# PEER stage: a comparison row in PSUM, 42 instead of 28 expert products made ahead, a quarter of the gated one-hots in VectorE alone

## The chip, the cores and the metric

The kernel runs on one core of a Trainium2 chip. The metric is the device time of one execution in microseconds (us), the median of three runs. TensorE multiplies matrices (PE in the rows, PEld for its weight loads), VectorE is DVE, ScalarE is ACT, GpSimd is POOL, and SyncE (SP) issues most of the DMAs. SBUF is the working memory of the engines, PSUM the memory that TensorE writes to, in eight banks.

## The reference, cut to what matters

The program is a transformer of several blocks over 512 tokens with 1024 features. Only its last layer, `peer_ffn`, is touched by the change:

```
q  = n @ w_q                      # 8 heads, 2 halves of 128
s  = q . sub_keys                 # 128 keys per head and half
s1, i1 = top_k(s[:, :, 0], 16);  s2, i2 = top_k(s[:, :, 1], 16)
cand   = s1 + s2 (16 x 16);      top_s, pos = top_k(cand, 16)
idx    = i1[...] * 128 + i2[...]  # one of 16384 experts
gate   = softmax(top_s)
act    = gelu(expert_u[idx] . n)
out    = sum over 8 heads x 16 experts of gate * act * expert_v[idx]
```

So each token takes 128 of 16384 experts, and the sum of their value rows is weighted with gate times activation.

## The kernel before, in words

The 512 tokens are handled in two ways. For the first 384 (`TD`, three blocks of 128, `ND` = 3) the layer is computed densely: all 16384 experts are gone through in 128 tiles of 128 (`NE`). For the last 128 tokens the rows of the chosen experts are fetched one by one with indirect DMAs. Everything is in float32. A matmul of float32 operands is made of three passes over a high and a low half (`acc3`, L154 to L160), so each weight tile is split on arrival (`wload`, L143, with `split`, L139): ScalarE copies the high half (L140), VectorE or GpSimd subtracts it for the low half (L141).

The layer has three stages.

- *Routing* (`route`, L1448 to L1532). For each head and half, TensorE makes the query (24 matmuls of 512 columns) and the scores, VectorE picks the best 16 (`top16`, L1397), combines the candidates (`second`, L1449) and recovers the chosen index: it compares positions with a row of numbers `iof` (L1474), GpSimd multiplies by the candidate index (L1476), VectorE sums (L1487).
- *Gates* (`gates`, L1537 to L1568). A matrix of gates, expert by token, is built for the 384 tokens. For each token two one-hot rows of 128 are made on VectorE by comparing the row `iof` with a token's index (L1548), in groups of four tokens, 96 groups in all; one of them is multiplied by the gate, on GpSimd in three groups of four (L1550) and on ScalarE in the fourth (L1553); TensorE multiplies the two (L1555) into PSUM tile `g`, ScalarE copies it out (L1559), and twelve DMAs on SP's queue store the gates to DRAM as `Gd` (L1563).
- *Gather* (`gather`, L1570 to L1698). For each expert tile i, `v_tile` (L1635) multiplies the expert product `hb` by the gates (L1649), splits the result, and TensorE accumulates it with the value weights into six PSUM banks (`v_block`, 18 matmuls of 512 columns, `acc`). Every fourth tile the next block of gates is loaded into the only buffer `g` (L1641). Row fetches for the last 128 tokens run beside it: an indirect DMA (L1612), a dot product (L1618) and a weighted addition (L1624) on VectorE. How many fetches go with a step follows from `done` (L1671): a step that has an expert product counts twice.

An *expert product* is `h_tile` (L1427): 24 matmuls of 384 columns on PSUM tiles `o` and `t` in turn, then a gelu on ScalarE (L1439). Products for i below `NA` = 10 stay in `early`, up to `NH` = 22 in twelve `hb` buffers; the next `NX` = 6 go through two buffers `away` to DRAM (L1441) and are loaded back in the gather stage (`h_back`, L1443). These 28 are made ahead: `NR` = 14 in the routing stage, one for each of the first 14 half heads, after the half head's scores, and 14 in the gates stage, one or two after every 32 tokens. The other 100 are made in the gather stage, each three steps (`LAG`) ahead of its v tile. Weights of products made ahead are split by GpSimd, the others by VectorE.

Each engine works through its own queue in order. The order on each queue is fixed when the program is built, and it is not quite that of the source: matmuls of an expert product stand between those of other tiles, and some products of the gates loop already lie in the routing stage. Weights are loaded through four buffers (`wr`) and split into four (`ws`), so a load can run up to four tiles ahead.

PSUM use: two banks for `o` and `t` throughout, four more in routing, four in the gates, six in the gather stage.

Of the kernel before, what the change touches and what calls it, by code (L numbers as in the profile page):

```python
# [56 lines left out]
class Net:  # L57
# [1348 lines left out]

    def peer(self, st):
        nc, V, S, G, T, I = self.nc, self.V, self.S, self.G, self.T, self.I
        ND, NE, NA, NH, NX, NR, NS = 3, 128, 10, 22, 6, 14, 4
        TD = ND * 128  # L1410
        u, rest, ws = self.start(st)
        pp = self.ctx.enter_context(self.tc.tile_pool(name="peer", bufs=1))
# [30 lines left out]
        def h_back(i):  # L1443

            hbs[i] = dn.tile([128, TD], F32, name="hb", bufs=NH - NA)
            nc.sync.dma_start(hbs[i], hs[i - NH])

        with self.phase("route") as rp, self.banks(mm=2, s=2):  # L1448
            def second(h, v16, i16):  # L1449

                if16 = rp.tile([128, 4, 2, 16], F32, name="if16", bufs=2)
                V.tensor_copy(if16, i16)
                V.tensor_scalar(if16[:, :, 0], if16[:, :, 0], 128.0, None, OP.mult)
                cs = rp.tile([128, 4, NCAND], F32, name="cs", bufs=2)
                ci = rp.tile([128, 4, NCAND], F32, name="ci", bufs=2)
                off = 0
                for i0, ni, nj in CAND:
                    n = ni * nj
                    for dst, src, e in ((cs, v16, V), (ci, if16, G)):
                        o = dst[:, :, off:off + n].rearrange("p h (a b) -> p h a b", b=nj)  # L1460
                        a_ = src[:, :, 0, i0:i0 + ni, None].to_broadcast([128, 4, ni, nj])
                        b_ = src[:, :, 1, None, 0:nj].to_broadcast([128, 4, ni, nj])
                        e.tensor_tensor(o, a_, b_, OP.add)
                    off += n
                tsc = rp.tile([128, 4, 16], F32, name="tsc", bufs=2)
                tpi = rp.tile([128, 4, 16], U32, name="tpi", bufs=2)
                for tb in range(4):
                    self.top16(tsc[:, tb], tpi[:, tb], cs[:, tb], NCAND)
                tpf = rp.tile([128, 4, 16], F32, name="tpf", bufs=2)
                V.tensor_copy(tpf, tpi)  # L1470
                eqs = []
                for tb in range(4):
                    eq = rp.tile([128, 16, NCAND], F32, name="eq", bufs=4)
                    V.tensor_tensor(eq, tpf[:, tb, :, None].to_broadcast([128, 16, NCAND]),  # L1474
                                    iof[:, None, 0:NCAND].to_broadcast([128, 16, NCAND]), OP.is_equal)
                    G.tensor_tensor(eq, eq, ci[:, tb:tb + 1].to_broadcast([128, 16, NCAND]), OP.mult)  # L1476
                    eqs.append(eq)
                g = gate[:, :, h]
                V.tensor_tensor(g, tsc, tsc[:, :, 0:1].to_broadcast([128, 4, 16]), OP.subtract)
                S.activation(g, g, AF.Exp)  # L1480
                gs = self.sm.tile([128, 4], F32, name="gs")
                V.tensor_reduce(gs, g, AX.X, OP.add)
                V.reciprocal(gs, gs)
                V.tensor_tensor(g, g, gs[:, :, None].to_broadcast([128, 4, 16]), OP.mult)
                yield
                for tb, eq in enumerate(eqs):
                    V.tensor_reduce(idf[:, tb, h], eq, AX.X, OP.add)  # L1487
                    yield

            late = []  # L1490
            Ps = [self.pt("mm"), self.pt("s")[:, 0:TD], self.pt("mm"), self.pt("s")[:, 0:TD]]
            first = self.gemm_first(ws, u, rest, (T_, TD, T_, TD), Ps)
            for h in range(8):
                v16 = rp.tile([128, 4, 2, 16], F32, name="v16", bufs=2)
                i16 = rp.tile([128, 4, 2, 16], U32, name="i16", bufs=2)
                for p in range(2):
                    j = 2 * h + p
                    key = rp.tile([128, 128], F32, name="key", bufs=2)
                    nc.sync.dma_start(key, I["keysT"][:, j * 128:(j + 1) * 128])
                    P = first.pop(0) if first else self.gemm_a([(I["peer_w_q"][j], 8)], u, G)  # L1500
                    hP = first.pop(0) if first else None
                    q = self.tmp.tile([128, T_], F32, name="qT", tag="sw", bufs=2)
                    S.activation(q, P, AF.Copy)
                    P = self.pt("s", (128, 4, 128))
                    for tb in range(4):
                        T.matmul(P[:, tb], q[:, tb * 128:(tb + 1) * 128], key, start=tb == 0, stop=tb == 3,
                                 skip_group_check=True)
                    sc = rp.tile([128, 4, 128], F32, name="sc", bufs=3)
                    S.activation(sc, P, AF.Copy)
                    for tb in range(4):  # L1510
                        self.top16(v16[:, tb, p], i16[:, tb, p], sc[:, tb], 128)
                    if p == 0 and late:
                        self.weave(late.pop())
                    if j < NR:
                        h_tile(j, hP)
                late.append(second(h, v16, i16))
                next(late[0])
            ei = rp.tile([128, 2, ND, NE], I32, name="ei", bufs=1)
            ef = rp.tile([128, 2, ND, NE], F32, name="ef", bufs=1)
            for tb in range(4):  # L1520
                next(late[0])
                e = ei[:, 0, tb] if tb < ND else idx
                V.tensor_copy(e, idf[:, tb].rearrange("p b c -> p (b c)"))
                if tb == ND:
                    break
                V.tensor_scalar(ei[:, 1, tb], e, 127, None, OP.bitwise_and)
                V.tensor_scalar(e, e, 7, None, OP.logical_shift_right)
                V.tensor_copy(ef[:, :, tb], ei[:, :, tb])
                P = self.pt("s", (128, 3, 128))
                for j in range(3):  # L1530
                    T.transpose(P[:, j], ef[:, j, tb] if j < 2 else gate[:, tb].rearrange("p a b -> p (a b)"), self.idf)
                S.activation(eT[:, :, tb * 128:tb * 128 + 128], P, AF.Copy)  # L1532
# [4 lines left out]
        with self.phase("gates") as rp, self.banks(g=4):  # L1537
            nh = NR
            for t0 in range(0, TD, 32):
                for t1 in range(0, 32, 8):  # L1540
                    P = self.bank[0].tile([128, 8, 128], F32, name="g", tag="g", bufs=2)
                    for k in range(0, 8, 4):
                        t = t0 + t1 + k
                        o = [self.tmp.tile([128, 4, 128], F32, name="o0", tag="tmp"),
                             rp.tile([128, 4, 128], F32, name="o1", bufs=4)]
                        col = lambda x: x[:, t:t + 4, None].to_broadcast([128, 4, 128])
                        for i in (1, 0):
                            V.tensor_tensor(o[i], iof[:, None].to_broadcast([128, 4, 128]), col(eT[:, i]), OP.is_equal)  # L1548
                        if t // 4 % NS:
                            G.tensor_tensor(o[1], o[1], col(gT), OP.mult)  # L1550
                        else:
                            for x in range(4):
                                S.activation(o[1][:, x], o[1][:, x], AF.Copy, scale=gT[:, t + x:t + x + 1])  # L1553
                        for x in range(4):
                            T.matmul(P[:, k + x], o[1][:, x], o[0][:, x], start=True, stop=True)  # L1555
                    if t1 == 0:
                        st = [rp.tile([128, 64, 32], F32, name="gst", bufs=3) for i in range(2)]
                    for i in range(2):
                        S.activation(st[i][:, :, t1:t1 + 8].rearrange("p a t -> p t a"),  # L1559
                                     P[:, :, i * 64:i * 64 + 64], AF.Copy)  # L1560
                S.activation(g_now[:, t0 // 32], st[0][:, 0:4], AF.Copy)
                for i in range(2):
                    nc.sync.dma_start(Gd[t0 // 32, i * 16:i * 16 + 16].rearrange("a b t -> b a t"),  # L1563
                                      st[i].rearrange("p (a x) t -> p a (x t)", x=4))
                n1 = NR + (NH + NX - NR) * (t0 // 32 + 1) // (TD // 32)
                for i in range(nh, n1):
                    h_tile(i)
                nh = n1  # L1568

        with self.phase("gather") as gp, self.banks(acc=6):  # L1570

            def nrm(*todo):
# [332 lines left out]
```

## Time and profile before

| | |
|---|---|
| median of three runs | 4230.45 us (4223.23 to 4231.51) |
| the profiled execution | 4224.36 us, span of its instructions 4222.5 us |
| routing, from 2832 to 3058 us | 226 us |
| gates, from 3058 to 3250 us | 192 us |
| gather, from 3250 to 4195 us, and the end to 4222.5 us | 945 and 27.5 us |

The profile is of one execution. "Busy" counts the time in which an engine runs an instruction; a wait inside an instruction counts as busy, and a matmul's recorded duration is longer than its distance from the next, since matmuls overlap. "Idle before" is the time an engine stood still before an instruction, put down to whatever ended last. [...] The boundaries of the stages above are read from the order of the instructions.

### The profile page before, as it was taken

The numbers are of one execution on the slowest core, as the hardware profiler recorded it, in microseconds if no ns is written. First come the engines' busy times: TensorE is split into PE (matmuls) and PEld (weight loads), VectorE is DVE, ScalarE is ACT, GpSimd is POOL, SyncE is SP. The second block draws the span as 40 slices with busy tenths as digits, with TensorE's granted clock in tenths as the row PEclk, the third lists the DMA queues.
The fourth block names the chain that finished last, engine by engine and source line by source line (L and its number), as shares of the span: only waits on it lengthen the run. The fifth ranks groups of instructions, "written<-read, shape, count | busy, mean of one in ns | idle before, by whom it ended". The sixth has DMA issues, their size and how long they took to land.

```text
span 4222.5 us, 54408 instructions
## 1 busy us (share of the span) xinstructions
PE 4015.4 (95%) x20388; PEld 3411.3 (81%) x20388; DVE 2822.3 (67%) x5043; ACT 1675.7 (40%) x3108; POOL 768.6 (18%) x573
## 2 busy tenths in 40 slices
PE   7999999999999999999999999798778999999999
PEld 5888789998888888885568889587667799999998
DVE  7556655666654575557664337969998777777777
ACT  3224443444322332245553224443366433433333
POOL 2001211110000100013010004337764011111111
PEclk9999999999999999999999999899999999999999
DMA  6654222322454446540023324032256788888886
GB/s 239 191 185 138 86 75 75 90 78 67 136 186 155 129 136 189 185 129 28 1 70 128 102 86 138 29 108 85 74 146 197 252 313 304 296 306 297 308 298 228
DMA packets 267896, 661.18 MB, mean 157 GB/s; under 512 B 24048, under 2 KB 126960, under 8 KB 250864
## 3 DMA queue, kind: packets, MB, share of 16 engines
q1 hardware_dynamic: 249200, 523.48, 38.5%
q0 software_dynamic: 18432, 134.23, 8.7%
q8 instruction: 160, 2.62, 0.3%
q14 instruction: 104, 0.85, 0.1%
HBM read 624.86 MB, written 32.77 MB: 156 GB/s over the span
## 4 chain that ended last, share of the span: by engine, by line
PE 75%; DVE 16%; issue 5%; DMA 2%; ACT 1%; POOL 1%; SPq 0%; DVEq 0%; ACTq 0%; POOLq 0%
PE mm L156 15%; PE mm L160 14%; PE mm L159 14%; PE acc L160 4%; PE acc L159 4%; PE acc L156 4%; DVE o L1548 3%; PE o L1104 2%; DVE cv L1242 2%; PE t L160 2%; PE t L156 2%; PE t L159 2%; PE o L160 2%; PE o L156 2%; PE o L159 2%
## 5 line engine op out<-in xcount | busy, mean ns | idle before, releaser
L141 DVE TENSOR_TENSOR wspl<-wraw,wspl 128x1024 fp32r<-128x1024 f32 (+3 forms) x695 | 787.1, 1135 | 707.1 <-ACT wspl L140 702.6
L140 ACT ACTIVATE wspl<-wraw 128x1024 fp32r<-128x1024 f32 (+3 forms) x757 | 746.4, 987 | 1156.7 <-PE mm L160 523.0
L156 PE MATMUL mm<-u,wspl 128*128 128x512 f32 (+1 forms) x1888 | 709.2, 379 | 14.9 <-ACT u L379 6.9
L160 PE MATMUL mm<-u,wspl 128*128 128x512 f32 (+1 forms) x1888 | 708.2, 376 | 1.3 <-POOL wspl L141 0.7
L159 PE MATMUL mm<-u,wspl 128*128 128x512 f32 (+1 forms) x1888 | 707.8, 375 | 0.2 <-DVE u L380 0.2
L156 PEld LDWEIGHTS mm<-u,wspl 128*128 128x128 f32 x1888 | 357.6, 190 | 82.4 <-ACT u L379 8.2
L160 PEld LDWEIGHTS mm<-u,wspl 128*128 128x128 f32 x1888 | 357.7, 190 | 66.3 <-POOL wspl L141 1.9
L159 PEld LDWEIGHTS mm<-u,wspl 128*128 128x128 f32 x1888 | 358.0, 190 | 63.6 <-DVE u L380 1.0
L244 POOL TENSOR_TENSOR ss<-sq,ss 128x256 f32<-128x256 f32 (+1 forms) x63 | 75.4, 1197 | 1563.9 <-ACT sq L241 1563.7
L160 PE MATMUL mm<-act,wspl 128*128 128x512 f32 (+1 forms) x880 | 307.5, 349 | 3.3 <-DVE wspl L141 3.3
L156 PE MATMUL mm<-wspl,u 128*128 128x512 f32 (+1 forms) x736 | 309.2, 420 | 1.1 <-ACT u L379 1.0
L156 PE MATMUL mm<-act,wspl 128*128 128x512 f32 (+1 forms) x880 | 307.4, 349 | 0.0
L159 PE MATMUL mm<-act,wspl 128*128 128x512 f32 (+1 forms) x880 | 305.5, 347 | 0.0
L156 PE MATMUL acc<-wspl,a 128*128 128x512 f32 x750 | 292.3, 390 | 5.3 <-ACT a L140 5.3
L160 PE MATMUL acc<-wspl,a 128*128 128x512 f32 x750 | 294.4, 393 | 1.2 <-DVE a L141 1.2
L1612 POOL DMA_INDIRECT uv<-in_peer_uv_dram,idx x128 | 152.0, 1187 | 787.7 <-DVE oq L1624 758.5
L159 PE MATMUL acc<-wspl,a 128*128 128x512 f32 x750 | 293.6, 392 | 0.0
L160 PE MATMUL mm<-wspl,u 128*128 128x512 f32 (+1 forms) x736 | 281.5, 383 | 1.7 <-DVE u L380 1.7
L159 PE MATMUL mm<-wspl,u 128*128 128x512 f32 (+1 forms) x736 | 281.5, 383 | 0.0
L543 DVE TENSOR_TENSOR silu<-silu,mm 128x512 f32<-128x512 f32 x88 | 60.2, 687 | 245.3 <-PE mm L160 212.6
L156 PEld LDWEIGHTS mm<-wspl,u 128*128 128x128 f32 x736 | 186.0, 253 | 21.6 <-issue 8.0
L160 PEld LDWEIGHTS mm<-wspl,u 128*128 128x128 f32 x736 | 185.7, 253 | 12.6 <-DVE u L380 1.9
(534 smaller groups left out, 8141.6 us busy)
## 6 DMA issues: line engine op xcount, KB each, us to landing
wraw<-in_ffn_w_in_dram SPq DMA_DIRECT2D x176, 512.0 KB
wraw<-in_w_adaT_dram SPq DMA_DIRECT2D x128, 512.0 KB
wraw<-in_peer_uT_dram SPq DMA_DIRECT2D x128, 512.0 KB
wraw<-in_peer_v_dram SPq DMA_DIRECT2D x128, 512.0 KB
wraw<-in_a_w_qkv_dram SPq DMA_DIRECT2D x72, 512.0 KB
wraw<-in_ffn_w_out_dram SPq DMA_DIRECT2D x80, 384.0 KB
wraw<-in_ffn_w_out_dram SPq DMA_DIRECT2D x80, 320.0 KB
Gd<-gst SPq DMA_DIRECT2D x24, 1024.0 KB
```

What stands on the lines that cost most here:

```text
L140: self.S.activation(dst_hi, src, AF.Copy)
L141: (eng or self.V).tensor_tensor(dst_lo, src, dst_hi.bitcast(F32), OP.subtract)
L156: x = self.T.matmul(P, a[0], b[0], start=start, stop=False)
L159: self.T.matmul(P, a[0], b[1], start=False, stop=False)
L160: self.T.matmul(P, a[1], b[0], start=False, stop=stop)
L244: (e or self.G).tensor_tensor(acc, t, acc, OP.add)
L543: self.V.tensor_tensor(s, s, Pu, OP.mult)
L1104: T.matmul(st["O"][par * 64:par * 64 + 64], lhsT, rhs, start=start, stop=stop, skip_group_check=True)
L1242: V.scalar_tensor_tensor(acc, gl[c][:, k:k + T_], w(k), acc, OP.mult, OP.add)
L1548: V.tensor_tensor(o[i], iof[:, None].to_broadcast([128, 4, 128]), col(eT[:, i]), OP.is_equal)
L1612: G.indirect_dma_start(out=r, out_offset=None, in_=I["peer_uv"], in_offset=bass.IndirectOffsetOnAxis(ap=idx[:, e:e + 1], axis=0))
```

## The change

- `iop`, a copy of the row `iof` in a PSUM bank, is held from before the routing stage to the end of the gates stage. The comparisons of L1474 and L1548 read it in place of `iof`.
- 42 expert products are made ahead in place of 28 (`NX` 20 in place of 6): 21 in routing (`NR`; 16 with the half heads, now before the scores, and five after the last head) and 21 in the gates stage, where they now follow every eight tokens and not every 32. Twenty go through DRAM in place of six.
- In the fourth group of each four of the gates, in place of a comparison and four scalings on ScalarE, four VectorE instructions of 128 columns compare and scale in one. The first one-hot is made after the gated one.

```
-        ND, NE, NA, NH, NX, NR, NS = 3, 128, 10, 22, 6, 14, 4
+        ND, NE, NA, NH, NX, NR, NS = 3, 128, 10, 22, 20, 21, 4
...
+        wide = ExitStack()
+        iop = wide.enter_context(self.tc.tile_pool(name="iop", bufs=1, space=PSUM, reuse_waits="tile")).tile([128, NE], F32, name="iop")
+        V.tensor_copy(iop, iof)
...
-                                    iof[:, None, 0:NCAND].to_broadcast([128, 16, NCAND]), OP.is_equal)
+                                    iop[:, None, 0:NCAND].to_broadcast([128, 16, NCAND]), OP.is_equal)
...
                     S.activation(q, P, AF.Copy)
+                    h_tile(j, hP)
...
-                    if j < NR:
-                        h_tile(j, hP)
                 late.append(second(h, v16, i16))
                 next(late[0])
+            for i in range(16, NR):
+                h_tile(i)
...
-                        for i in (1, 0):
-                            V.tensor_tensor(o[i], iof[:, None].to_broadcast([128, 4, 128]), col(eT[:, i]), OP.is_equal)
                         if t // 4 % NS:
+                            V.tensor_tensor(o[1], iop[:, None].to_broadcast([128, 4, 128]), col(eT[:, 1]), OP.is_equal)
                             G.tensor_tensor(o[1], o[1], col(gT), OP.mult)
                         else:
                             for x in range(4):
-                                S.activation(o[1][:, x], o[1][:, x], AF.Copy, scale=gT[:, t + x:t + x + 1])
+                                V.tensor_scalar(o[1][:, x], iop, eT[:, 1, t + x:t + x + 1], gT[:, t + x:t + x + 1],
+                                                OP.is_equal, OP.mult)
+                        V.tensor_tensor(o[0], iop[:, None].to_broadcast([128, 4, 128]), col(eT[:, 0]), OP.is_equal)
...
+                    n1 = NR + (NH + NX - NR) * (t0 + t1 + 8) // TD
+                    for i in range(nh, n1):
+                        h_tile(i)
+                    nh = n1
...
-                n1 = NR + (NH + NX - NR) * (t0 // 32 + 1) // (TD // 32)
-                for i in range(nh, n1):
-                    h_tile(i)
-                nh = n1
+        wide.close()
```

## Rows read from the trace of the kernel before

**Rows 1.** The page, part 1: busy us of each engine, share, instructions.

```profile
PE 4015.4 (95%) x20388; PEld 3411.3 (81%) x20388; DVE 2822.3 (67%) x5043; ACT 1675.7 (40%) x3108; POOL 768.6 (18%) x573
```

**Rows 2.** Busy times by stage: stretch, its us, engines (instructions), clock, DMA share, GB/s.

```profile
2832.00:3058.00 226.00, 184.18 (x940) 164.57 (x939) 216.50 (x964) 84.05 (x114) 164.00 (x123) 0.92 0.26 84
3058.00:3250.00 192.00, 147.63 (x971) 133.86 (x970) 185.56 (x188) 133.12 (x220) 115.31 (x79) 0.94 0.52 150
3250.00:4195.00 945.00, 938.36 (x4693) 843.35 (x4692) 701.97 (x871) 368.95 (x706) 150.05 (x127) 1.00 0.85 296
```

**Rows 3.** Groups by line in the gates stage: busy us, mean ns, idle before.

```profile
L1548 DVE TENSOR_TENSOR o<-iof,eT 128x512 f32<-128x512 f32 x185 | 181.7, 1057 | 4.0 <-PE g L1555 4.0
...
L1553 ACT ACTIVATE o<-o,eT 128x128 f32<-128x128 f32 x96 | 31.7, 389 | 15.6 <-DVE o L1548 15.1
L141 POOL TENSOR_TENSOR wspl<-wraw,wspl 128x1024 fp32r<-128x1024 f32 x6 | 16.4, 2736 | 8.6 <-ACT wspl L140 8.6
...
L140 ACT ACTIVATE wspl<-wraw 128x1024 fp32r<-128x1024 f32 x8 | 8.4, 1054 | 0.0
...
L1439 ACT ACTIVATE away<-t 128x384 f32<-128x384 f32 x3 | 1.4, 477 | 0.0
```

**Rows 4.** The lines L1548 and L1474: durations, ns, minimum/median/maximum.

```profile
L1548 DVE TENSOR_TENSOR o<-iof,eT x192: 676/680/2868, 3052.1 to 3242.8; 128x512 f32<-128x512 f32 x192
...
L1474 DVE TENSOR_TENSOR eq<-tpf,iof x32: 970/1755/2555, 2855.0 to 3038.6; 128x800 f32<-128x800 f32 x32
```

**Rows 5.** In order of time near 67 us, GpSimd and VectorE: start, us, instructions.

```profile
66.33 4.78 POOL L141 TENSOR_TENSOR wspl<-wraw,wspl 128x1024 fp32r<-128x1024 f32 x2 [25.57 <-ACT wspl L140]
...
67.72 1.88 DVE L543 TENSOR_TENSOR silu<-silu,mm 128x512 f32<-128x512 f32 x3 [3.67 <-ACT silu L541]
```

**Rows 6.** Lines L543, L585 and L847: durations, ns, minimum/median/maximum.

```profile
L543 DVE TENSOR_TENSOR silu<-silu,mm x88: 674/687/691, 67.7 to 2512.4; 128x512 f32<-128x512 f32 x88
...
L585 DVE TENSOR_TENSOR kk<-kk,ropeC x8: 273/278/561, 1502.9 to 1528.9; 128x128 f32<-128x128 f32 x8
...
L847 DVE SCALAR_TENSOR_TENSOR wp<-phi,cols,wp x30: 332/352/931, 1461.2 to 1517.9; 128x128 f32<-128x128 f32 x30
```

**Rows 7.** Busy times of three stretches of the gather stage.

```profile
3266.00:3296.00 30.00, 30.00 (x134) 24.86 (x133) 16.11 (x28) 12.57 (x18) 0.00 (x0) 1.00 0.66 207
3315.00:3365.00 50.00, 46.54 (x200) 36.51 (x198) 38.01 (x52) 19.81 (x35) 7.34 (x6) 1.00 0.86 290
3400.00:4190.00 790.00, 790.00 (x3996) 719.20 (x3995) 597.53 (x722) 310.26 (x607) 133.85 (x114) 1.00 0.86 302
```

**Rows 8.** Waits in the gates stage: total us, times, longest; then SP's queue.

```profile
PEld g L1555 <- POOL o L1550: 24.9, 30, 2.1
PEld g L1555 <- ACT gst L1559: 24.0, 15, 2.4
...
DVE o L1548 <- PE g L1555: 4.0, 2, 2.9
...
SPq L1563 <- ACT gst L1559: 69.1, 12, 13.3
```

**Rows 9.** Waits between 3295 and 3370 us, in the gather stage.

```profile
DVE x L1649 <- DMA g<-Gd: 13.1, 4, 4.3
```

**Rows 10.** SP's queue in order of time: first and last of four loads of gates.

```profile
3301.13 0.38 SPq L1641 DMA_DIRECT2D g<-Gd  x1
...
3356.42 0.38 SPq L1641 DMA_DIRECT2D g<-Gd  x1
```

**Rows 11.** DMA queue of row fetches (packets, MB); issues from 3250 to 3400 us.

```profile
q0 software_dynamic: 18432, 134.23, 8.7%
...
wraw<-in_peer_v_dram SPq DMA_DIRECT2D x26, 512.0 KB
g<-Gd SPq DMA_DIRECT2D x7, 768.0 KB
...
hb<-hs SPq DMA_DIRECT2D x6, 192.0 KB
```

## The prediction

> **What bounds the kernel now.** I read four views in this order. The page first: TensorE is busy for 95% of the span, so a gain must take work or gaps from TensorE [rows 1]. Then the busy times by stage, because the share hides three stages with different limits [rows 2]. In the routing stage (226 us) VectorE is busy for 216.5 us and TensorE for 184.2; in the gates stage (192 us) VectorE shows 185.6 us (the rest are seams between its instructions) and TensorE 147.6; in the gather stage (945 us) TensorE is busy for 938.4 and VectorE for 702.0. So the first two stages are VectorE's, with 41.8 + 44.4 = 86 us in which TensorE stands still, and the third is TensorE's.
>
> Third, what VectorE does in the gates. Its comparisons at L1548 are nearly all of it: 181.7 us in that window, at a mean of 1057 ns [rows 3]. The form by itself has a minimum of 676 and a median of 680 ns, but a maximum of 2868 [rows 4]: half of them are quick, and the rest wait inside themselves. The routing comparison at L1474 does the same: 970 at best, 1755 in the median [rows 4]. What runs beside both is GpSimd's multiplication. So VectorE's bound in both stages is partly a bound by contention. Where VectorE reads one operand from PSUM, the trace shows no such stretch: near 67 us three comparable instructions (L543, the product read from PSUM) run in 1.88 us together under two GpSimd splits of 2.4 us each [rows 5], and all 88 of that line lie at 674 to 691 ns [rows 6].
>
> [...]
>
> Fourth, the gather stage in pieces [rows 7]. With products only of the second kind (v tiles: 18 matmuls each) and no fetches, 134 matmuls take 30 us, 0.224 us each, 4.03 us a tile. In the steady part one v tile and one expert product (24 matmuls) come in turn: 3996 matmuls in 790 us, 0.1977 us each, 8.30 us for 42, so an expert product takes 8.30 - 4.03 = 4.27 us; I use 4.2, since a few records can be missing. Between them, where v tiles run alone with row fetches beside them, TensorE is busy for 46.5 of 50 us.
>
> **Part 1, the comparison row moves to PSUM.** Routing: 32 comparisons go from their mean near 1.76 us to about 0.98 (the minimum of the same form plus a little), 32 x 0.78 = 25 us off VectorE. Gates: 192 comparisons, at 1057 ns by their mean [rows 3], become 96 for the first one-hot and 72 for the second, 168 x 0.687 = 115 us, with L543's duration as the price. That PSUM operand's price is 687 against 680 ns, 7 ns, or 1.4 us over all 200.
>
> [...]
>
> The copy that fills the PSUM row is one short instruction at the head of the stage. VectorE can wait in it for a free bank (seven of eight are then in use), and the splits for the first products queue behind it: 0 to 2.9 us, the longest wait of VectorE for a PSUM result in the gates [rows 8]. I take 0.3.
>
> **Part 2, a quarter of the gated one-hots in VectorE.** 24 of 96 groups drop one comparison and four ScalarE scalings (31.7 us off ScalarE) and add four 128-wide instructions each, 96 in all. No row has a 128-wide scalar form from PSUM. Nearest: 273 ns for a 128-wide two-tensor product without contention, 352 for one with a pointer scalar [rows 6]. I take 300 ns: 29 us (26 to 34). VectorE in the gates: 115 + 29 = 144 us in place of 186.
>
> **Part 3, 14 more products made ahead.** Seven go to routing and seven to the gates. They leave the gather stage, where TensorE is the bound: 14 x 4.2 = 59 us. They arrive where TensorE has gaps. The two earlier stages then hold, over 418 us: TensorE 184.2 + 147.6 + 59 = 391 us, VectorE 216.5 - 25 + 185.6 - 42 = 335 us. GpSimd has 164 + 115 + 14 more splits x 2.7 = 317, if its own multiplications don't get shorter; ScalarE gains 14 x (1.05 + 0.48) = 21 us and loses 31.7 [rows 3]. So the bound of the two stages passes from VectorE to TensorE, at 391 us plus its gaps, less what the clock gives back: the granted clock was 0.92 and 0.94 there against 1.00 in the gather stage [rows 2]. [...] Both ends: 373 us (no gap, full clock) and 418 + 59 = 477 (every product on top of what there is). I take 396: today's 86 us of gaps shrink to some 15, as they end on late operands that GpSimd and ScalarE hand over (24.9 and 24.0 us of weight-load waits [rows 8]) in a stage that VectorE no longer paces, and the clock returns 10. That is 22 us less than 418.
>
> Every moved product brings a weight load, a ScalarE and a GpSimd half of the split, an activation and a store to DRAM on SP's queue, and in the gather stage a load back (192 KB instead of 512 KB of weights). On SP the stores stand among the 12 stores of gate blocks, which hold the queue for 69.1 us waiting for ScalarE [rows 8]; weight loads behind them are four buffers ahead, so this stays hidden at one product per 9 us. If that cover went, the longest single wait of these, 13.3 us, could fall to TensorE at each of 12 blocks.
>
> **Part 4, the longer stretch of v tiles alone.** It grows from 25 to 39 tiles, and 14 of the new ones lie where row fetches run beside. There the gate block for four tiles has one buffer: the load goes out only after the last use, and VectorE waited 13.1 us for it in 4 loads [rows 9], four that leave from 3301.13 to 3356.42 us, 18.4 us apart [rows 10], against 4 x 4.03 = 16.1 of TensorE work. So each group of four costs 2.3 us over TensorE's pace, and 3.5 more groups 8 us. More data move there too: a v tile 0.52 MB, a quarter of a gate block 0.20, a reloaded product 0.20, and 0.64 fetched rows (128 of 200 steps' weight) of 134.23 / 128 = 1.05 MB, 1.59 MB in all, 6.4 MB a group [rows 11]; in 18.4 us that is 346 GB/s against the 290 measured. I add 2 us for a slower landing. Gather stage: 59 - 8 - 2 = 49 us less (55 to 38).
>
> **The sum.** 22 + 49 = 71 us. The profiled execution took 4224.36 us (span 4222.5 and 1.9 around it): 4153. The median of the runs, 4230.45, lies 6 us above it: 4159, written 4160.
>
> **Rivals.**
> (a) The PSUM row doesn't free VectorE, so the change doesn't do what it says. Then routing stays 226 us and the gates become 168 x 1.057 + 29 = 207 us, 15 longer than now; the gather gain stands: 49 - 15 = 34 off, 4196. For it: none of the rows has this form with a broadcast row in PSUM. Against it: rows 5 and 6.
> (b) The stretch of v tiles alone becomes bound by data. At the 302 GB/s of the steady part [rows 7], the highest that a long stretch shows, a group takes 6.4 / 302 = 21.1 us, 2.7 more than now over 27 / 4 = 6.75 groups, 18 us in place of my 2: 4176. For it: the demand of 346. Against it: 302 is what that part asked for, not what it was refused, as TensorE was busy throughout.
> (c) Slower: TensorE's gaps stay. Its queue is in order, and a product behind a matmul that waits for a one-hot waits too; if the gaps of 86 us are kept and the 14 products come on top, the two stages take 477 us, 59 more, against 49 saved: 10 us slower, 4240. It decides from 49 us not hidden, that is once the gaps shrink by less than 10 of their 86 us. For it: the gaps end on hand-overs that also exist after the change. Against it: VectorE's relief of 25 + 42 us is what those hand-overs wait for.
>
> **How the numbers follow.** Forecast 4160, chance 0.62, its own range 4135 to 4185. (a) 0.12, (b) 0.14, (c) 0.12, of which 0.05 between 0.2% either way and 0.07 slower. A difference under 0.2%, 8 us, can't be told from none here. Faster: 0.62 + 0.12 + 0.14 = 0.88. The low end takes both favourable bounds: 418 - 373 = 45 and 55, 100 us, 4130. The high end takes in (a) with the worse price of the scalar forms and the slower gather, 8 us above it: 4204. Outside lie (c) and a little of the rest.
>
> **What would show it.** Right: L1548's successors at about 0.69 us whatever GpSimd does, the routing comparison at 1.0; VectorE busy well under the gates stage's length; TensorE busy over 93% in both early stages with a granted clock nearer 1.00; 39 v tiles in a row with a wait for the gate block about every 18 us; the steady part 59 us shorter. Wrong: comparisons above 0.8 us, an early stage longer than now, or VectorE's waits for the gate block above 4 us each.

## The result

The changed kernel takes 4159.0 us in the median (4150.9 to 4166.3), the kernel before 4230.2 beside it: a ratio of 0.9835 with a 95% interval of 0.9813 to 0.9856, 71 us less. The profiled execution took 4150.94 us, with a span of 4149.2 against 4222.5.

Busy times of the changed kernel by stage (columns as in rows 2); the gates stage now lies from 3030 to 3222 us:

```profile
2832.00:3030.00 198.00, 180.83 (x961) 163.86 (x961) 192.54 (x966) 82.33 (x113) 152.98 (x127) 0.97 0.30 101
3030.00:3222.00 192.00, 177.76 (x1262) 174.43 (x1262) 133.32 (x259) 124.62 (x148) 115.98 (x89) 0.98 0.67 201
3222.00:4122.00 900.00, 885.30 (x4355) 788.47 (x4354) 683.85 (x856) 350.70 (x679) 165.34 (x127) 0.99 0.86 305
```

Against [rows 2], routing is 28 us shorter, and VectorE's busy time there is 24 us less. The gates take 192 us as before, but with another engine in front: VectorE falls from 185.6 to 133.3 us, TensorE rises from 147.6 to 177.8. The gather stage is 45 us shorter. TensorE's standing time in the first two stages is 17 + 14 = 31 us in place of 86, and the granted clock there is 0.97 and 0.98 in place of 0.92 and 0.94. That clock is TensorE's, as a share of its full speed; the traces of both kernels hold records at 1.00 and at 0.50, the lower level, and at no other. The products' matmuls of 384 columns start 173 ns apart in the median at 1.00 and 320 at the lower level (before), the v tiles' of 512 columns 227 and 427 (changed kernel).

The comparisons of the changed kernel, with the line of the scalar form (minimum, median and maximum in ns; L1477 is the routing comparison, L1552 and L1558 those of the gates, L1556 the quarter):

```profile
L1477 DVE TENSOR_TENSOR eq<-tpf,iop x32: 980/981/991, 2851.7 to 3010.2; 128x800 f32<-128x800 f32 x32
...
L1552 DVE TENSOR_TENSOR o<-iop,eT x72: 679/681/690, 3028.0 to 3212.4; 128x512 f32<-128x512 f32 x72
...
L1556 DVE TENSOR_SCALAR o<-iop,eT x96: 401/402/411, 3026.1 to 3209.1; 128x128 f32<-128x128 f32 x96
...
L1558 DVE TENSOR_TENSOR o<-iop,eT x96: 679/683/692, 3027.4 to 3215.3; 128x512 f32<-128x512 f32 x96
...
L1553 POOL TENSOR_TENSOR o<-o,eT x72: 1029/1040/1887, 3028.8 to 3213.2; 128x512 f32<-128x512 f32 x72
```

Where [rows 4] reach 2868 and 2555 ns, nothing now exceeds 692 and 991. GpSimd's multiplication has a median of 1040 ns.

The stretch in which v tiles run alone, and two parts of it:

```profile
3226.00:3411.00 185.00, 173.08 (x749) 140.06 (x749) 127.56 (x183) 66.56 (x115) 25.68 (x18) 0.96 0.83 284
3325.00:3350.00 25.00, 20.56 (x85) 16.58 (x84) 17.10 (x23) 8.75 (x16) 3.63 (x3) 0.93 0.93 322
3375.00:3400.00 25.00, 22.27 (x81) 17.43 (x82) 17.45 (x24) 8.57 (x16) 3.70 (x3) 0.84 0.69 242
```

Its waits from 3222 to 3412 us (total, times, longest):

```profile
DVE x L1655 <- DMA g<-Gd: 22.9, 7, 4.9
...
PE acc L156 <- ACT a L140: 13.4, 6, 4.4
```

TensorE stands still for 12 us of 185, and at two places the granted clock has dropped, to 0.93 and 0.84. VectorE's wait for the block of gates is 22.9 us here, in seven waits, against 13.1 in four from 3295 us on in the shorter stretch of before [rows 9].

### The profile page after: what moved, and what is told of

Its sections match the earlier page's. It is cut to its first block, busy times and chain, and to the rows that moved or that the text cites. A ratio compares the mean times of both kernels' runs of the same rounds, so it can differ in the third digit from the quotient of the medians.

```text
span 4149.2 us, 54488 instructions
## 1 busy us (share of the span) xinstructions
PE 3988.8 (96%) x20388; PEld 3395.6 (82%) x20388; DVE 2729.2 (66%) x5102; ACT 1649.2 (40%) x3012; POOL 775.2 (19%) x587
## 5 line engine op out<-in xcount | busy, mean ns | idle before, releaser
L141 DVE TENSOR_TENSOR wspl<-wraw,wspl 128x1024 fp32r<-128x1024 f32 (+3 forms) x681 | 769.4, 1133 | 658.7 <-ACT wspl L140 651.2
L1618 POOL DMA_INDIRECT uv<-in_peer_uv_dram,idx x128 | 166.5, 1300 | 728.8 <-DVE oq L1630 700.6
L543 DVE TENSOR_TENSOR silu<-silu,mm 128x512 f32<-128x512 f32 x88 | 60.3, 687 | 252.4 <-PE mm L160 229.8
L141 POOL TENSOR_TENSOR wspl<-wraw,wspl 128x1024 fp32r<-128x1024 f32 x76 | 188.1, 2487 | 162.0 <-ACT wspl L140 156.2
L156 PEld LDWEIGHTS mm<-wspl,u 128*128 128x128 f32 x736 | 185.7, 252 | 21.6 <-issue 8.0
```

What stands on the lines that cost most here:

```text
L141: (eng or self.V).tensor_tensor(dst_lo, src, dst_hi.bitcast(F32), OP.subtract)
L156: x = self.T.matmul(P, a[0], b[0], start=start, stop=False)
L543: self.V.tensor_tensor(s, s, Pu, OP.mult)
L1618: G.indirect_dma_start(out=r, out_offset=None, in_=I["peer_uv"], in_offset=bass.IndirectOffsetOnAxis(ap=idx[:, e:e + 1], axis=0))
```

## The experiments

Lengths of the stages in us, read from TensorE's instructions in the trace of one execution of each kernel: routing from the first score matmul to the first gate matmul, gates from there to the first v tile, the v tiles alone up to the first expert product among them, and the rest to the end. What lies ahead of the first score matmul is left out: that matmul starts at anything from 2829 to 2844 us, so that small differences are read better from the stages than from the medians. The median of the kernel before was 4227 to 4230 us beside each.

| kernel | median us | routing | gates | v tiles alone | rest |
|---|---|---|---|---|---|
| before | 4230.2 | 221.0 | 196.6 | 113.9 | 853.7 |
| changed | 4159.0 | 196.7 | 195.1 | 185.5 | 737.7 |
| 1 row in SBUF | 4230.3 | 219.2 | 240.4 | 193.3 | 737.7 |
| 2 row only | 4176.5 | 198.2 | 166.6 | 117.4 | 853.7 |
| 3 28 ahead | 4179.8 | 193.1 | 169.2 | 119.1 | 853.7 |
| 4 no gating | 4194.4 (one) | 221.1 | 161.9 | 115.4 | 853.7 |
| 5 ScalarE quarter | 4165.1 | 195.6 | 201.5 | 188.3 | 737.7 |
| 6 coarse | 4160.2 | 196.5 | 191.9 | 189.7 | 737.7 |
| 7 two gate blocks | 4135.0 | 196.5 | 195.0 | 164.8 | 737.7 |
| 8 its control | 4160.3 | 196.7 | 194.5 | 192.9 | 737.7 |
| 9 35 ahead | 4153.4 | 196.5 | 182.8 | 137.8 | 795.7 |
| 10 25 in routing | 4139.8 | 203.5 | 192.6 | 166.4 | 737.7 |
| 11 28 ahead, 21 in routing | 4160.6 | 197.2 | 159.5 | 109.3 | 854.2 |
| 12 four store buffers | 4131.3 | 196.5 | 190.8 | 166.0 | 737.7 |

### 1. The row in SBUF again, the rest of the change kept

```
-                                    iop[:, None, 0:NCAND].to_broadcast([128, 16, NCAND]), OP.is_equal)
+                                    iof[:, None, 0:NCAND].to_broadcast([128, 16, NCAND]), OP.is_equal)
...
-                                V.tensor_scalar(o[1][:, x], iop, eT[:, 1, t + x:t + x + 1], gT[:, t + x:t + x + 1],
+                                V.tensor_scalar(o[1][:, x], iof, eT[:, 1, t + x:t + x + 1], gT[:, t + x:t + x + 1],
```

(and the two comparisons of the gates likewise)

> The changed kernel with the comparison row read from SBUF again; the 42 products made ahead, their fine spreading and the quarter of the gated one-hots in VectorE stay. Theory (the PSUM row frees VectorE from waiting for GpSimd): the routing comparison goes back from 0.98 to 1.7 us or more and the gates comparison from 0.68 to about 1.05; routing is again about 225 us, the gates 200 to 215 us, the gather stage keeps its 45 us of gain, so 4195 us in all (4180 to 4215). Rival (the row does nothing, the moved products alone fill TensorE's gaps): 4160 us, within 8.

Measured: 4230.3 us, ratio 1.0004 (0.9990 to 1.0019), no different from before. The rival falls. The theory's direction holds, but its range of 4180 to 4215 was missed: the gates take 240 us and not 200 to 215, and the gather stage is shorter than before by 37 us and not by 45. Its gates stage, and the lines there:

```profile
3058.00:3299.00 241.00, 200.03 (x1274) 192.35 (x1272) 208.83 (x269) 128.13 (x151) 163.47 (x91) 0.91 0.56 167
```

```profile
L1552 DVE TENSOR_TENSOR o<-iof,eT x72: 673/679/2875, 3058.8 to 3283.6; 128x512 f32<-128x512 f32 x72
...
L1556 DVE TENSOR_SCALAR o<-iof,eT x96: 331/336/2473, 3055.7 to 3280.3; 128x128 f32<-128x128 f32 x96
...
L1553 POOL TENSOR_TENSOR o<-o,eT x72: 1032/1356/4299, 3059.5 to 3287.7; 128x512 f32<-128x512 f32 x72
```

The comparisons stretch to 2.9 us again, and so does the new scalar form: the 51 of them that had no GpSimd instruction beside them in time took 331 to 338 ns, the 45 that had one 1056 to 2473. GpSimd's multiplication has one of 4.3 us, where the longest in the changed kernel is 1.9. So the run undoes two things at once, the row of the comparisons and that of the quarter. The 96 scalar forms keep VectorE busy for 74 us here, at a mean of 832 ns; the 24 comparisons whose place they took would be 25 us at the 1057 ns of [rows 3]. What the run shows is that without the PSUM row the 14 moved products and the quarter together are worth nothing: 44 us go into the gates, 37 come out of the gather stage. The products without the row and without this form were not run, so how much of the 44 us is theirs stays open.

### 2. The row alone

```
+        iop = wide.enter_context(self.tc.tile_pool(name="iop", bufs=1, space=PSUM, reuse_waits="tile")).tile([128, NE], F32, name="iop")
+        V.tensor_copy(iop, iof)
...
-                            V.tensor_tensor(o[i], iof[:, None].to_broadcast([128, 4, 128]), col(eT[:, i]), OP.is_equal)
+                            V.tensor_tensor(o[i], iop[:, None].to_broadcast([128, 4, 128]), col(eT[:, i]), OP.is_equal)
```

(and the routing comparison likewise)

> The kernel before with nothing changed but the row in PSUM. Theory: routing falls by the 25 us of its 32 comparisons, from 226 to about 200; in the gates VectorE falls from 186 to about 133 us, and the stage to what TensorE, GpSimd and ScalarE need with their hand-overs, about 160 us (145 to 175); the gather stage as before; 4230 - 26 - 32 = 4172 us (4155 to 4190). That would leave only some 13 us to the moved products. Rival (row without effect): 4222 to 4238. Second rival (only routing is bound by VectorE, the gates by other hand-overs): 4205.

Measured: 4176.5 us, ratio 0.9879 (0.9863 to 0.9896): 52 us, and 73% of the whole gain, from the row alone, inside the theory's range. The comparison and the stage:

```profile
L1551 DVE TENSOR_TENSOR o<-iop,eT x192: 677/679/693, 3027.4 to 3190.8; 128x512 f32<-128x512 f32 x192
```

```profile
3031.00:3198.00 167.00, 138.68 (x989) 125.55 (x987) 118.91 (x193) 132.35 (x224) 88.76 (x78) 0.99 0.61 174
```

VectorE falls from 185.6 to 118.9 us in the gates. The stage ends up with no engine over 139 of 167 us. Of the 28 us in which TensorE stands still, 24 end on one-hots or copies that ScalarE (19) and GpSimd (5) hand over.

### 3. The change with 28 products ahead

```
-        ND, NE, NA, NH, NX, NR, NS = 3, 128, 10, 22, 20, 21, 4
+        ND, NE, NA, NH, NX, NR, NS = 3, 128, 10, 22, 6, 14, 4
...
-                    h_tile(j, hP)
+                    if j < NR:
+                        h_tile(j, hP)
```

> The changed kernel with 28 products made ahead again (14 in routing, 14 in the gates, spread as finely as in the changed kernel; six through DRAM). Theory: the gather stage returns to 945 us, the gates shrink from 192 to about 160 as seven products of 4.2 us leave a stage that TensorE now fills to 93%, routing stays near 198; 4172 us (4155 to 4190), so 42 products bring about 13 us. Rival (the moved products bring what the gather stage shows, 45 us, at no price in the stages before): 4204 us.

Measured: 4179.8 us, ratio 0.9886 (0.9869 to 0.9903). The 14 more products bring 21 us on top of the row, where the theory had 13: 49.6 in the gather stage, less 29.5 in the two before. With the run before, all of the change but the products is worth no more than the row by itself.

### 4. The kernel before without GpSimd's gating

```
-                        if t // 4 % NS:
-                            G.tensor_tensor(o[1], o[1], col(gT), OP.mult)
-                        else:
+                        if t // 4 % NS == 0:
```

> The kernel before, with the row in SBUF, and without GpSimd's multiplication by the gate in three of four groups of the gates stage: those one-hots stay without their gate, so that part of the sum is left out and what it costs isn't in the time. Theory (the comparisons wait for GpSimd's reads, whatever memory the row is in): L1548's mean falls from 1.04 to 0.70 us with both operands in SBUF, a few still stretched by the six weight splits on GpSimd. Rival (a comparison with a broadcast row in SBUF is slow by itself): its mean stays above 0.95 us.

The comparison's line, and the gates stage:

```profile
L1548 DVE TENSOR_TENSOR o<-iof,eT x192: 675/681/2877, 3056.5 to 3211.6; 128x512 f32<-128x512 f32 x192
```

```profile
3061.00:3223.00 162.00, 133.60 (x985) 123.66 (x983) 129.60 (x191) 131.99 (x224) 16.52 (x7) 1.00 0.65 188
```

With both operands in SBUF and GpSimd nearly silent, VectorE is busy for 129.6 us in the stage, and the same 192 comparisons take 0.74 us in the mean in place of 1.04. Single ones still reach 2.9 us, as GpSimd's 16.5 us of weight splits stay: the 179 that had no GpSimd instruction beside them took at most 0.69 us. The stage takes 162 us, close to the 167 of run 2: taking GpSimd's multiplications away and taking VectorE's second SBUF operand away do much the same to it, though this run has one hand-over less as well. Its total is of one execution and isn't used. The cause is the two together, not the form of the comparison.

### 5. The quarter on ScalarE again

```
-                                V.tensor_scalar(o[1][:, x], iop, eT[:, 1, t + x:t + x + 1], gT[:, t + x:t + x + 1],
-                                                OP.is_equal, OP.mult)
+                                S.activation(o[1][:, x], o[1][:, x], AF.Copy, scale=gT[:, t + x:t + x + 1])
```

(after one comparison of all four from the PSUM row)

> The changed kernel with the quarter of the gated one-hots made as before, by one comparison (from the PSUM row) and four ScalarE scalings. Theory (this part only moves 32 us from ScalarE to VectorE, and neither paces the gates any longer): VectorE loses 96 x 0.40 - 24 x 0.68 = 22 us, ScalarE gains 32 and comes to some 158 of 195 us; the gates 193 to 203 us; 4156 to 4168 us. Rival (ScalarE's hand-overs pace the gates, so its relief was needed): the gates grow by 15 us or more, 4175.

Measured: 4165.1 us, ratio 0.9857 (0.9841 to 0.9873), the changed kernel 0.9835 (0.9813 to 0.9856): the intervals overlap. The gates are 6 us longer. The quarter is worth some 6 us, if anything, and the theory, that neither engine paces the stage, holds within that.

### 6. The products of the gates stage placed after every 32 tokens

```
-                    n1 = NR + (NH + NX - NR) * (t0 + t1 + 8) // TD
+                n1 = NR + (NH + NX - NR) * (t0 // 32 + 1) // (TD // 32)
```

(with the loop that follows moved out by one level)

> The changed kernel with the products of the gates stage placed as before, one or two after every 32 tokens in the source. Theory (the order on TensorE's queue is not the source's, so the place matters little): within 6 us of the changed kernel, 4153 to 4167. Rival (the fine spreading is what lets 21 products fit): the gates grow by 15 us or more, 4175 and over, with single waits of TensorE above 4 us at the block ends.

Measured: 4160.2 us, ratio 0.9843 (0.9826 to 0.9859); the gates 191.9 us. The fine spreading in the source does nothing that can be seen here.

### 7 and 8. Two buffers for the block of gates, and the control

```
-        ND, NE, NA, NH, NX, NR, NS = 3, 128, 10, 22, 20, 21, 4
+        ND, NE, NA, NH, NX, NR, NS = 3, 128, 10, 18, 24, 21, 4
...
-        gtile = lambda: dn.tile([128, 12, 4, 32], F32, name="g")
+        gtile = lambda: dn.tile([128, 12, 4, 32], F32, name="g", bufs=2)
```

(the control has the first line alone)

> The changed kernel with two buffers for the block of gates in the gather stage; to make room, four of the twelve product buffers are given up (NH 18 and NX 24, so 42 products ahead as before, 24 and not 20 through DRAM). Theory (the stretch of v tiles alone loses its time to the one buffer: a load that starts only after the last use): VectorE's waits for the block go from 26 us to under 5, the 39 tiles take 165 to 172 us in place of 185, and the whole 4143 us (4135 to 4150). Rival (that stretch is bound by data, over 320 GB/s): it stays above 180 us and other waits take the place of this one; 4155 us or more.

> The control for the run with two gate blocks: the changed kernel with NH 18 and NX 24 and one buffer for the block of gates. Both theories: as the changed kernel, 4155 to 4168 us, as eight product buffers still lead the v tiles by more than the three steps that are needed and four more products of 192 KB go out and come back.

Measured: 4135.0 us, ratio 0.9779 (0.9763 to 0.9796), against 4160.3 and 0.9843 (0.9826 to 0.9859) for the control: 25 us from the second buffer, at the low end of what the theory said. The stretch of v tiles alone with two buffers, and a part of it:

```profile
3233.00:3398.00 165.00, 164.90 (x751) 137.27 (x752) 128.95 (x184) 66.63 (x116) 23.82 (x19) 1.00 0.94 329
3333.00:3358.00 25.00, 25.00 (x112) 20.67 (x112) 22.20 (x30) 11.27 (x22) 3.70 (x3) 1.00 1.06 386
```

TensorE has no gap in it, the clock stays at 1.00, the wait for `g` is gone, and the same data pass at 329 GB/s in the mean and 386 over 25 us. So the stretch was bound by the one buffer and not by data: rival (b) falls.

### 9 to 11. How many products, and in which stage (all with two gate blocks)

```
-        ND, NE, NA, NH, NX, NR, NS = 3, 128, 10, 18, 24, 21, 4
+        ND, NE, NA, NH, NX, NR, NS = 3, 128, 10, 18, 17, 21, 4
```

(run 9; run 10 has NX 24 and NR 25, run 11 NX 10 and NR 21)

> Two gate blocks, 35 products ahead: 21 in routing as in the changed kernel, 14 and not 21 in the gates (NH 18, NX 17). Theory (a product in the gates costs 4.1 us there, as 14 against 21 showed, 167 against 195 us, so it is worth nothing; only those in routing are free): gates 167 us, the stretch of v tiles alone 7 tiles of 4.08 us shorter, the steady part 58 us longer: 4136 us (4129 to 4143), no different from 42 ahead with two blocks, 4135. Rival (a product in the gates saves its 4.2 us of the gather stage): 4164 us.

> Two gate blocks, 42 products ahead, 25 of them in routing and 17 in the gates. Theory (in routing VectorE paces at 193 of 197 us and TensorE is busy for 180, so 17 us of products are still free there): gates 195 to 179 us, routing longer by 0 to 6 us; 4123 us (4117 to 4131). Rival (TensorE's gaps in routing are of its in-order queue and can't be filled): routing grows by the 17 us and nothing is gained, 4135.

> Two gate blocks, 28 products ahead, 21 of them in routing and 7 in the gates (NH 18, NX 10). Theory (4.1 us for a product in the gates as long as TensorE paces that stage; below some 145 us VectorE's 134 us and the hand-overs do): gates 145 to 155 us, against 139 were the price to go on; 4142 to 4155 us. Rival (the price stays 4.1 us down to seven products): 4137 us.

Measured: 4153.4, 4139.8 and 4160.6 us. All three theories missed, and so did their rivals. In run 9 the gates take 183 us and not 167: a product there is neither free nor without worth. The reason for the miss shows when the products' matmuls are counted in the traces rather than in the source, since the order on TensorE's queue is another: between the first gate matmul and the first v tile lie 8.5 products before, 20.3 in the changed kernel, 8.7 in run 2, 7.6 in run 3, 13.3 in run 9, 16.3 in run 10 and 6.3 in run 11. From run 11 (6.3, 159.5 us) to run 7 (20.3, 195.0 us) that is 2.5 us for a product in the mean, against 4.2 in the gather stage; by run 9 the first seven of the 14 cost 23 us and the other seven 12. In run 10, four products more in routing cost 7 us there, though TensorE had 17 us to spare, and four fewer in the gates give back 2.4: TensorE then is busy for 193 of 203 us in routing.

```profile
2838.00:3041.00 203.00, 193.38 (x1040) 176.10 (x1040) 194.70 (x964) 87.49 (x121) 158.10 (x128) 1.00 0.35 114
3041.00:3234.00 193.00, 168.37 (x1172) 162.68 (x1171) 137.56 (x264) 121.49 (x143) 107.67 (x87) 0.96 0.65 191
```

The gates keep 193 us with TensorE at 168, so what paces them is not TensorE's time alone.

### 12. Four buffers for the gates on their way out

```
-        ND, NE, NA, NH, NX, NR, NS = 3, 128, 10, 18, 24, 21, 4
+        ND, NE, NA, NH, NX, NR, NS = 3, 128, 10, 14, 28, 21, 4
...
-                        st = [rp.tile([128, 64, 32], F32, name="gst", bufs=3) for i in range(2)]
+                        st = [rp.tile([128, 64, 32], F32, name="gst", bufs=4) for i in range(2)]
```

> Two gate blocks and four, not three, buffers for the gates on their way to DRAM; to make room four product buffers are left (NH 14, NX 28, so 42 products ahead, 21 in routing). Theory (ScalarE waits 15.6 us in the gates for a store to leave its buffer, 9 times, and that is what lies between TensorE's 178 us and the stage's 195): that wait goes, the gates take 182 to 188 us, 4125 us (4118 to 4130) against 4135 with three buffers. Rival (the stage's rest is the hand-over of one-hots from GpSimd to TensorE, 10 us of waits, and ScalarE's wait is beside the path): gates 193 to 197 us, 4131 to 4140. If four product buffers are too few for a lead of three steps, the steady part grows over 738 us, which is to be read apart from the gates.

Measured: 4131.3 us, ratio 0.9768 (0.9754 to 0.9781), the fastest of all, though not apart from run 7 (0.9779, 0.9763 to 0.9796). Waits in its gates stage:

```profile
ACT gst L1564 <- PE g L1560: 26.6, 30, 5.2
...
PEld g L1560 <- POOL o L1553: 12.5, 6, 3.3
PE g L1560 <- POOL o L1553: 10.8, 6, 2.9
...
PEld g L1560 <- ACT gst L1564: 0.6, 2, 0.3
```

ScalarE's wait for a store (15.6 us in run 7) is gone, and the gates are 4 us shorter: most of that wait lay beside the path. What is left on TensorE is the wait for GpSimd's one-hots. The 190.8 us lie between the theory's 182 to 188 and the rival's 193 to 197, and the steady part stays at 738 us, so four product buffers are enough. What else holds the gates at 191 us with TensorE busy for 178 wasn't settled.

## Why the prediction was right, and where its steps were off

**The total.** 4160 was forecast, 4159.0 came; 4153 for the profiled execution, 4150.9 came. Errors of the terms partly cancelled: the early stages gave 26 us in place of 22 and the gather stage 44.5 in place of 49. That the sum meets the median within 1 us is luck.

**The comparisons.** Forecast 0.687 and 0.98 us; 0.68 and 0.98 came, so rival (a) falls. The long comparisons of [rows 4] were read rightly as waits for GpSimd. Set beside GpSimd's instructions in time, 76 of the 192 before took over 0.72 us and all 76 had one beside them, while the 48 that had none took 677 to 682 ns; in the changed kernel 142 of 168 had one, and none was stretched. Run 4 shows the other half of it. The forecast's own evidence was thinner than it looks: of the 88 instructions of L543 only three had a GpSimd instruction beside them. The routing stage is 24 us shorter by the table, and VectorE's busy time in it by as much (25 forecast).

**The quarter.** The scalar form was put at 300 ns (273 to 352) and takes 402. The term was mis-sized: 39 us of VectorE in place of 29. VectorE had room for it, 133 of 192 us. In run 1, with its row in SBUF, the same form takes 336: that is the price of the PSUM row here, 66 ns. What makes it up, the runs don't show. The two-operand comparison paid 1 to 3 ns for its PSUM row, with medians of 681 and 683 ns in place of 680.

**The early stages.** Forecast: TensorE 391 us busy, gaps of 15 and 10 us given back by the clock, 396 us, 22 less. No run shows the 18 us between the 391 and the lower end of 373, from which the 10 are taken; what the trace before shows is 43 us of TensorE's busy time at the lower level, by the 320 and 173 ns of the matmuls some 20 us lost (an estimate). By the windows there are 390 us, 28 less, of which 3 us lie ahead of the first score matmul (at 2837.3 us before, 2834.1 after) and belong to the spread of that point; by the table it is 26 less. The sum is near, its terms are not: TensorE is busy for 359 us, and stands still for 31, twice the 15 of the sum. The busy time of the products' matmuls grew by some 54 us and not 59; the gate matmuls, taken at their old busy time of 110 us, take 95 in the same 768 records; and the clock returned more than forecast: TensorE was busy at the lower level for 43 us before and for 13 after, and of the difference 14 us (an estimate from the same 320 and 173 ns) came back in place of 10. These overlap, as a part of what the gate matmuls lost is the clock's. The bound didn't pass to TensorE as the step said: in the gates no engine holds it alone, as run 10 shows. One sign of being right came only in part with it: TensorE is busy for 91.3 and 92.6% of the two stages, where over 93% was named.

**Where the products went.** Seven to each stage was read from the source. In the trace 2.2 of the 14 went to routing (17.5 to 19.7) and 11.8 to the gates.

**The gather stage.** Forecast 49 us less, 44.5 came (first v tile to the end). The price of a product, 4.2 us, was right: the steady part is 853.7 - 737.7 = 116 us shorter for 14 steps, 8.29 each, less 4.09 for a v tile (run 7: 164.8 us, less 5.3 for the addition of the input, over 39). The stretch of v tiles alone was under-priced. Against 4.09 us a tile it lost 6 us before and 21 after, 14 more in place of the 10 forecast. The mechanism was the one named, the single block buffer, as run 7 shows; two of the seven waits for it, 4.9 and 4.5 us, are above the 4 us that was named as a sign of being wrong. But the sum has no term for the clock in this stretch: TensorE stands still for 12 us in it, 8 more than before, and the granted clock of 0.96, which was 1.00 in the same stretch before, makes up some 6 us of the 185, an estimate from the 12.3 us that TensorE was busy there at the lower level and the 427 and 227 ns.

**What made the gain.** The sum credits the gather stage with 49 of 71 us. Run 2 gives the row 52 us with the products where they were; run 3 gives the products 21 us on top of the row, and run 1 gives them nothing without it, together with the quarter in SBUF. Run 4 and the rows of runs 1 and 2 show the mechanism: the row opens room in the early stages, and the products fill it at about 2.5 us in place of 4.2. The forecast had both parts and their sum, but not that the room is worth nearly as much empty.

**Rival (c)**, the products on top of what there is, comes near to what run 1 shows: 44 us into the gates, 37 out of the gather stage, though a part of the 44 is the quarter's form in SBUF. With the row it didn't come. Its premise, that a product behind a waiting gate matmul waits too, shows in the trace before: a product on `t` had begun at 3128.04 us, with its weights split, and went on at 3138.55, after gate matmuls, though TensorE stood still from 3135.02 to 3137.27 until ScalarE had copied `g` out.

## What to carry to other kernels

When an instruction's median is far below its mean, or like the routing comparison's far above its minimum, look for what runs beside it before pricing its engine as the bound: here one operand moved to PSUM freed two engines (in the gates of run 2 VectorE was busy for 118.9 us in place of 185.6, GpSimd for 88.8 in place of 115.3) and brought 52 us. Work that is moved into an earlier stage is worth the difference of its prices in the two stages, 4.2 against 2.5 us here, and it must be counted where the queues put it, not where the source does. A stage that is made longer by such a move shows its next limit, here a single buffer whose second copy was worth as much as the 14 products.

## What the runs showed of the hardware

- The wait was mutual. GpSimd's multiplication of 128x512 fell from a median of 1356 ns (run 1) to 1040, and the routing multiplication from 2.28 to 1.76 us in the mean, once VectorE had one SBUF operand.
- A one-tensor scalar form of VectorE in SBUF was hit as well: 336 ns in the median, 2473 at most (run 1); from PSUM 402 and 411, though 77 of its 96 had a GpSimd instruction beside them.
- A lower clock went with short stops of TensorE, though not with every one. In the changed kernel's stretch of v tiles the granted clock is 0.96, in single parts 0.93 and 0.84: it fell to the lower level three times, at 3337, 3375 and 3399 us, around the ends of TensorE's three longest stops there, 4.4, 3.3 and 1.6 us. In run 7, where TensorE has no gap in that stretch, it is 1.00 for the same work; in the kernel before, whose stops there were at most 1.1 us, it is 1.00 too. A stop of 2.6 us in the changed kernel just before the stretch, up to 3226 us, was followed by no fall.
